# Score products over 64 rows and over 128: the lower parts of the keys in tiles of their own, beside zeros

## The chip, the cores and the metric

The kernel runs on one core of a Trainium2 chip. A core has a matrix engine (TensorE, PE in the profile, its weight loads shown apart as PEld), three engines for element-wise work (VectorE or DVE, ScalarE or ACT, GpSimd or POOL) and one that issues DMAs (SyncE, SP). The metric is the device time of one execution in microseconds (us).

## The reference, cut to what matters

Two layers of an encoder, 512 tokens, model width 1024, all in float32. Each layer is a feed-forward half (SwiGLU, inner width 2816), then three mixers side by side on the same normalised tokens, gated and summed, then a second feed-forward half. The mixers:

```
A: differential attention, 4 heads, two score maps per head over 64 features each
   sc = q[m] . k[m] * 64**-0.5 - slope * |t - s|      (m = 0, 1; 512 x 512)
   o  = softmax(sc[0]) v - lambda * softmax(sc[1]) v
B: windowed attention, 8 query heads, 2 key heads, 64 features, |t - s| <= 128
C: latent attention, 4 heads: sc = qn . kn (128 features) + qpe . kpe (64 rotary features, one kpe for all heads)
```

## The kernel before

Tokens lie along the free dimension (512 columns), features along the 128 partitions. Every float32 operand of a product is split in two parts of a type that TensorE takes in one pass: an upper part (hi, a rounded copy made by ACT) and a lower one (lo, the rest, a subtraction on DVE). A plain product is three products, hi·hi, hi·lo and lo·hi, summed in one PSUM bank (`mm3`, L155 to L157). The weights stream from memory through one queue in chunks of 128x1024 and are split on the way (L71, L72).

Scores over 64 features are done with two products and not three. Two heads (the two maps of A, the two key heads of B) lie in one tile, 64 rows each. `stacked` (L203) makes of the queries one tile per head, with the upper part in the head's own 64 rows and the lower part in the other 64. `doubled` (L217) makes of the keys one tile per head with the upper part in both halves, and one tile `lo` for both heads, each head's lower part in its own 64 rows. `mm_stacked` (L232) then forms the scores of 128 queries:

```
own = slice(m * 64, m * 64 + 64)
self.nc.tensor.matmul(ps, q[:, c], kh, start=start, stop=False)          # L235: 128 rows, (q hi + q lo) . k hi
self.nc.tensor.matmul(ps, q[own, c], kl[own], start=False, stop=stop)    # L236: 64 rows, q hi . k lo
```

In C the 128 unrotated features are three products at L702, and the rotary ones follow by `mm_stacked` into the same bank. The shared rotary key, pk, holds the same 64 features in both halves and is split once (`split`, L240 and L241) into kpeh and kpel.

A mixer runs head by head and step by step (`heads`). In A and C a step is a block of 128 queries against all 512 keys, four steps per head; A has two score maps per step. In B a step is two blocks of queries against the two or three blocks of keys in reach (256 or 384 columns), for two heads, two steps per pair of heads. A step's scores come first; the softmax runs on DVE and ACT (C: L705 to L710); then the step before is finished: its probabilities are transposed (L462), split, and multiplied with the values (L471 to L473, in B L659 to L662). Between the steps stand the projections of the next head and other projections and merges, as filling work. The order written in the code gives priorities; a planner fixes each engine's order of instructions when the program is built, from its own estimate of durations, and each engine keeps that order, waiting where an operand or a buffer isn't ready. POOL does the squares of the norms (L257 to L261, L545), the reciprocal roots (L274) and some sums. Tiles of 128x512 come from one pool of 72 "units"; a new one waits until one is free.

Of the kernel before, what the change touches and what calls it, by code (L numbers as in the profile page):

```python
# [16 lines left out]
P = 128  # L17
D = 1024
T = 512
# [20 lines left out]
class Stream:  # L40
    """The weights, 128 rows by 128 columns at a time, in the order of their use."""

# [44 lines left out]
    def fit(self, width):  # L87
        """Fills a chunk that has no room for so wide a block."""
        while self.pos % CH + width > CH:
            self.order.append((None, P))  # L90
            self.pos += P


class Kernel:
    RAW, AHEAD, WB = 3, 2, 3  # chunks of weights: buffers as loaded, loads ahead, buffers of their parts
    UNITS, PTS = 72, 4  # tiles of 512 and of 1024 columns
    WARM = 8  # products of zeros that raise TensorE's clock while the first loads are under way
    LAG = 1  # steps between the scores of a block of queries and the rest
    FILL0, RATES = (0, 1), (0.35, 0.6, 0.85)  # how much other work goes between an attention's steps

# [11 lines left out]

    # ---- tiles
    def u(self, dt=F32, shape=(P, T), name="u"):
# [26 lines left out]

    # ---- pieces
    def lookup(self, *args, **kw):
        """An activation that needs a table of its own; these keep their order, so that tables change seldom."""
        if self.last is None:
            self.last = self.nc.scalar.activation(*args, **kw)
        else:
            with self.tc.issue_after(self.last.ins):
                self.last = self.nc.scalar.activation(*args, **kw)

    def mm3(self, ps, w, x, start, stop):
        """ps += w^T x, each float32 as the sum of two parts that one pass carries."""
        (wh, wl), (xh, xl) = w, x
        mm = self.nc.tensor.matmul
        mm(ps, wh, xh, start=start, stop=False)  # L155
        mm(ps, wh, xl, start=False, stop=False)  # L156
        mm(ps, wl, xh, start=False, stop=stop)  # L157

    def proj(self, ps, src, xs):
        """128 output features for all tokens; src(k) names a block of weights."""  # L160
        n = len(xs)
        for k in range(n):
            self.mm3(ps, self.w.take(src(k)), xs[k], k == 0, k == n - 1)
# [15 lines left out]
    def group(self, pss, srcs, xs):  # L179
        """Several projections side by side, so that the last of xs is needed late. With no xs,  # L180
        they are made on the way from x."""
        n = len(xs) or NT
        for k in range(n):
            for ps, src in zip(pss, srcs):
                while len(xs) < min(k + (1 if ps is pss[0] else 3), n):
                    xs.append(self.gsplit(self.x[len(xs)], self.g(0, G_FFN1, len(xs)), "h"))
                self.mm3(ps, self.w.take(src(k)), xs[k], k == 0, k == n - 1)
            yield

    def group_rstd(self, pss, srcs, xs, at=(4, 6)):  # L190
        """A group, with the scale of the tokens worked out meanwhile."""
        res = g = None
        for k, _ in enumerate(self.group(pss, srcs, xs), 1):
            if k in at:
                g = g or self.rstd(self.sqacc, D, self.att)
                try:
                    next(g)
                except StopIteration as e:
                    res = e.value
        return res  # L200
# [4 lines left out]
    def stacked(self, src, name):  # L205
        """The parts of two heads' rows, each head's one above the other: the first head's with the
        upper part on top, the second's with the lower one."""
        out = []
# [8 lines left out]
    def doubled(self, src, name):  # L217
        """Of two heads' rows, each head's upper part twice above each other, and the lower parts."""
        out = []
        lo = self.u(F32R, name=name + "l")  # L220
        for m in range(2):
# [5 lines left out]
        for m in range(2):  # L227
            own = slice(m * 64, m * 64 + 64)
            self.nc.vector.tensor_tensor(lo[own], src[own], out[m][own].bitcast(F32), ALU.subtract)
        return out, lo  # L230

    def mm_stacked(self, ps, q, m, c, kh, kl, start, stop):  # L232
        """ps += q^T k over 64 rows: q as stacked, the upper part of k twice above each other."""
        own = slice(m * 64, m * 64 + 64)
        self.nc.tensor.matmul(ps, q[:, c], kh, start=start, stop=False)  # L235
        self.nc.tensor.matmul(ps, q[own, c], kl[own], start=False, stop=stop)  # L236

# [9 lines left out]
    def gsplit(self, src, g, name="g"):  # L247
        """The parts of src times a gain per partition."""
        hi, lo = self.pair(name)
# [13 lines left out]
    def rstd(self, acc, dim, bank, evac=True):  # L263
        """From sums of squares: 1/rms per token, down the partitions and across them. Yields
        where TensorE would wait."""
        nc = self.nc
# [17 lines left out]

    # ---- set-up
    def setup(self):
# [48 lines left out]

    # ---- feed-forward
    def next_h(self, j, gcol):
        """x's tile j is final: its part of the next norm's input."""
        h = None if gcol is None else self.gsplit(self.x[j], gcol, "h")
        if j == 0:  # L340
            self.sqacc = self.u(name="sqacc")
        self.square_sum(self.sqacc, self.x[j], j == 0)
        return h
# [67 lines left out]

    # ---- the three mixers
    def scaled(self, ps, R, by=None):
# [7 lines left out]
    def rproj(self, src, xs, R, by=None):  # L421
        """A projection of normalised tokens: the scale of a token comes after the product."""
        ps = self.acc()
# [6 lines left out]
    def vproj(self, xs, src, out, banks):  # L430
        """Values with tokens down the partitions, 512 features wide."""
        pss = [b("pv") for b in banks]
# [25 lines left out]
    def flip(self, p, n, hi, lo):  # L458
        """The parts of p's transposed blocks; hi and lo take n blocks side by side."""
        ps = self.att("tp")  # L460
# [4 lines left out]
    def pv(self, ps, v, pth, ptl):  # L465
        """ps += values^T probabilities^T over four blocks of keys, for two blocks of queries."""
        mm = self.nc.tensor.matmul
# [7 lines left out]
    def full_pv(self, hd, qb, d, v, st):  # L475
        """Transposes the probabilities of a block of queries; after two blocks, their products with the values."""
        if qb == 0:
# [12 lines left out]
    def heads(self, n, steps, prepare, first, second):  # L490
        """All heads' steps in one line: scores of a step, then the rest of the step before; the
        next head's projections in between. Yields where other work may go."""
        todo = []
# [17 lines left out]
    def branch_a(self, l, h, R, qk, out):  # L511
# [3 lines left out]
        def first(hd, qb):  # L515
# [3 lines left out]
            for m in range(2):  # L519
                self.mm_stacked(pss[m], q[m], m, slice(qb * P, (qb + 1) * P), k[0][m], k[1], True, True)  # L520
            ps = []
# [53 lines left out]
    def vproj_b(self, l, h, R, v):  # L575
        """Values of both key heads, each head's parts side by side."""
        t = yield from self.win(l, [(2176, P)], h, R)
# [16 lines left out]
    def branch_b(self, l, v, kk, h, R, qs, out):  # L594
# [5 lines left out]
        def first(j, hf):  # L600
# [6 lines left out]
            for qi in range(2):  # L607
# [5 lines left out]
                for m in range(2):  # L613
                    self.mm_stacked(pss[m][:, 0:n], q[m], m, slice(qb * P, (qb + 1) * P), kk[0][m][:, ks], kk[1][:, ks], True, True)
                for m in range(2):
# [21 lines left out]
        def second(j, hf, ps):  # L637
# [5 lines left out]
            for m in range(2):  # L643
# [6 lines left out]
                yield  # L650
                # above, the upper parts of the values; below, the lower ones
                side = slice(m * 256, m * 256 + 256)
# [40 lines left out]
    def branch_c(self, l, v, kpe, low, qk, out):  # L693
# [3 lines left out]
        def first(hd, qb):  # L697
# [3 lines left out]
            for i, (a, b) in enumerate(((0, 0), (0, 1), (1, 0))):  # L701
                nc.tensor.matmul(ps, q[a][:, c], k[b], start=i == 0, stop=False)  # L702
            self.mm_stacked(ps, qpe[hd % 2], hd % 2, c, *kpe, False, True)
            nm, s = self.small([P, 1], "cnm"), self.small([P, 1], "cs")
# [35 lines left out]
    def mix(self, l):  # L740
# [26 lines left out]
        z2, z0, z1 = [], [], []  # L767
        # compressed projections of C
        cols = [[(2688 + i * P, P)] for i in range(2)] + [[(2944, 64), (2976, 32), (2944, 32)]] + [[(2304 + i * P, P)] for i in range(3)]
# [34 lines left out]
        nc.tensor.matmul(pk, self.selr, krl, start=False, stop=True)  # L804
        kpe = self.split(pk, "kpe")
        RC, RS = self.u(name="RC"), self.u(name="RS")
# [66 lines left out]
def gather(order, nch, inp):  # L873
    """The weights' blocks, in the order of their use."""
    out = np.zeros((P, nch * CH), np.float32)
# [86 lines left out]
```

## Time and profile before

| | |
|---|---|
| time, median of 3 runs (lowest, highest) | 2548.37 us (2548.07, 2548.67) |
| span of the profiled execution, first to last instruction | 2544.7 us |
| mean granted TensorE clock | 0.998 of full speed |
| PE busy | 2524.1 us, 99% of the span, 11424 products |
| weight loads busy | 2044.0 us, 80% |
| DVE, ACT, POOL busy | 53%, 37%, 11% |
| score products L235 and L236 | 160 of 128 rows, 160 of 64 rows |

The profile is of one execution. PE's busy share says little, because products overlap: a plain one of 512 columns lasts 390 ns in the rows, and the next one starts before it has ended. What a product costs is the time from its start to the next one's start. A row of a timeline gives the start in us, the duration in us, engine, line, operation, tiles (written <- read), the sizes, and in brackets idle time of the engine just before and what ended it; "issue" means that nothing in the profile explains it.

### The profile page before, as it was taken

How to read it: one execution, taken by the hardware profiler on the slowest of the kernel's cores; microseconds unless marked ns; L12 is line 12 of the kernel's file. 1: busy time of each engine (PE TensorE's matmuls, PEld its weight loads, DVE VectorE, ACT ScalarE, POOL GpSimd, SP SyncE). 2: the span in 40 equal slices, each digit the busy share in tenths (PEclk: the TensorE clock that was granted, in tenths of full speed). 3: DMA queues.
4: the chain of work that ended last, by engine and by line, in shares of the span. 5: the costliest groups of instructions: out<-in, count | busy, mean ns of one | idle time of the engine just before them, and what ended most of it. 6: DMA issues, size and time to landing. Idle time of an engine off the chain costs nothing.

```text
span 2544.7 us, 28509 instructions
## 1 busy us (share of the span) xinstructions
PE 2524.1 (99%) x11424; PEld 2044.0 (80%) x11424; DVE 1355.1 (53%) x2004; ACT 936.2 (37%) x1429; POOL 270.6 (11%) x208
## 2 busy tenths in 40 slices
PE   9999999999999999999999999999999999999997
PEld 7888887777777888888888888877777788888886
DVE  6444336666667554443344443366666676544433
ACT  4332223365555433332233322244655553322211
POOL 4000123000001220001100001130000014100011
PEclk9999999999999999999999999999999999999999
DMA  4333332112212233333333333321222122333331
GB/s 159 93 97 100 95 122 86 59 58 75 67 58 67 88 94 100 93 97 100 95 96 100 93 98 99 106 81 51 67 75 66 56 70 89 102 97 94 100 99 67
DMA packets 62484, 223.22 MB, mean 88 GB/s; under 512 B 7200, under 2 KB 7344, under 8 KB 62352
## 3 DMA queue, kind: packets, MB, share of 16 engines
q1 hardware_dynamic: 60912, 217.67, 27.6%
q0 software_dynamic: 864, 2.70, 0.3%
q8 instruction: 89, 1.46, 0.2%
q10 hardware_dynamic: 576, 1.05, 0.1%
q14 instruction: 43, 0.35, 0.0%
HBM read 219.29 MB, written 2.10 MB: 87 GB/s over the span
## 4 chain that ended last, share of the span: by engine, by line
PE 95%; DVE 3%; ACT 1%; issue 1%; POOL 0%; DMA 0%; SPq 0%; DVEq 0%; POOLq 0%; ACTq 0%
PE pa L157 7%; PE pa L155 7%; PE pa L156 7%; PE acc L155 7%; PE po L155 6%; PE po L157 6%; PE po L156 6%; PE acc L156 6%; PE acc L157 6%; PE pg L156 5%; PE pg L155 5%; PE pg L157 5%; PE tp L462 2%; PE pm L155 2%; PE pm L157 2%; PE pm L156 2%
## 5 line engine op out<-in xcount | busy, mean ns | idle before, releaser
L72 DVE TENSOR_TENSOR wlo<-wraw,whi 128x1024 fp32r<-128x1024 f32 (+1 forms) x410 | 526.8, 1285 | 641.9 <-ACT whi L71 640.7
L71 ACT CAST whi<-wraw 128x1024 fp32r<-128x1024 f32 (+1 forms) x410 | 429.7, 1049 | 820.0 <-PE po L156 254.4
L155 PE MATMUL pa<-hh,whi 128*128 128x512 f32 x800 | 312.6, 391 | 0.9 <-DVE x L851 0.9
L157 PE MATMUL pa<-hh,wlo 128*128 128x512 f32 x800 | 311.7, 390 | 1.0 <-DVE wlo L72 1.0
L156 PE MATMUL pa<-hl,whi 128*128 128x512 f32 x800 | 311.7, 390 | 0.0
L155 PE MATMUL acc<-hh,whi 128*128 128x512 f32 x672 | 275.4, 410 | 0.0
L156 PE MATMUL acc<-hl,whi 128*128 128x512 f32 x672 | 263.9, 393 | 0.0
L157 PE MATMUL acc<-hh,wlo 128*128 128x512 f32 x672 | 263.5, 392 | 0.0
L155 PE MATMUL pg<-hh,whi 128*128 128x512 f32 x608 | 236.5, 389 | 0.0
L156 PE MATMUL pg<-hl,whi 128*128 128x512 f32 x608 | 236.5, 389 | 0.0
L157 PE MATMUL pg<-hh,wlo 128*128 128x512 f32 x608 | 236.5, 389 | 0.0
L155 PE MATMUL po<-ah,whi 128*128 128x512 f32 x576 | 224.1, 389 | 0.0
L156 PE MATMUL po<-al,whi 128*128 128x512 f32 x576 | 224.1, 389 | 0.0
L157 PE MATMUL po<-ah,wlo 128*128 128x512 f32 x576 | 224.1, 389 | 0.0
L155 PEld LDWEIGHTS pa<-hh,whi 128*128 128x128 f32 x800 | 150.4, 188 | 33.2 <-DVE x L851 1.3
L157 PEld LDWEIGHTS pa<-hh,wlo 128*128 128x128 f32 x800 | 150.3, 188 | 33.1 <-DVE wlo L72 1.9
L156 PEld LDWEIGHTS pa<-hl,whi 128*128 128x128 f32 x800 | 150.3, 188 | 31.2 <-DVE hl L251 0.3
L155 PEld LDWEIGHTS acc<-hh,whi 128*128 128x128 f32 x672 | 126.3, 188 | 32.5 <-issue 9.0
L157 PEld LDWEIGHTS acc<-hh,wlo 128*128 128x128 f32 x672 | 126.2, 188 | 27.7 <-issue 0.2
L156 PEld LDWEIGHTS acc<-hl,whi 128*128 128x128 f32 x672 | 126.6, 188 | 22.3 <-issue 0.9
L155 PEld LDWEIGHTS pg<-hh,whi 128*128 128x128 f32 x608 | 114.2, 188 | 23.8
L157 PEld LDWEIGHTS pg<-hh,wlo 128*128 128x128 f32 x608 | 114.1, 188 | 23.7
(248 smaller groups left out, 3906.5 us busy)
## 6 DMA issues: line engine op xcount, KB each, us to landing
wraw<-in_w SPq DMA_DIRECT2D x408, 512.0 KB, 3.5
x<-in_x SPq DMA_DIRECT2D x8, 256.0 KB, 6.4
rope<-in_rope POOLq DMA_DIRECT2D x6, 256.0 KB, 3.7
out<-o ACTq DMA_DIRECT2D x4, 256.0 KB, 2.9
out<-o SPq DMA_DIRECT2D x4, 256.0 KB, 3.4
dist<-in_cst POOLq DMA_DIRECT2D x1, 448.0 KB, 4.0
wraw<-in_w SPq DMA_DIRECT2D x1, 384.0 KB, 4.6
lv<-in_lam POOLq DMA_DIRECT2D x1, 256.0 KB, 3.9
```

Of the source, the lines that this page charges most:

```text
L71: self.k.nc.scalar.copy(hi[:, part], r[:, part])
L72: self.k.nc.vector.tensor_tensor(lo[:, part], r[:, part], hi[:, part].bitcast(F32), ALU.subtract)
L155: mm(ps, wh, xh, start=start, stop=False)
L156: mm(ps, wh, xl, start=False, stop=False)
L157: mm(ps, wl, xh, start=False, stop=stop)
L462: self.nc.tensor.transpose(ps[:, i * P:(i + 1) * P], p[:, i * P:(i + 1) * P], self.ident)
```

## The change

`doubled` gives each head's lower part a tile of its own, and the head's other 64 rows of that tile are filled with zeros by POOL (`beside_zeros`). The second product of `mm_stacked` then reads all 128 rows of the stacked queries and of this tile; the queries' lower part meets zeros. C's shared rotary key is no longer split by `split` but into one upper tile and two lower ones, one for each parity of heads, with two subtractions over 64 rows. Nothing else of the program changes; docstrings and comments are dropped.

```diff
     def doubled(self, src, name):
-        out = []
-        lo = self.u(F32R, name=name + "l")
+        out, low = [], []
         for m in range(2):
             t = self.u(F32R, name=name)
             own, other = slice(m * 64, m * 64 + 64), slice(64 - m * 64, 128 - m * 64)
@@
         for m in range(2):
             own = slice(m * 64, m * 64 + 64)
+            lo = self.beside_zeros(m, name + "l")
             self.nc.vector.tensor_tensor(lo[own], src[own], out[m][own].bitcast(F32), ALU.subtract)
-        return out, lo
-
-    def mm_stacked(self, ps, q, m, c, kh, kl, start, stop):
-        own = slice(m * 64, m * 64 + 64)
+            low.append(lo)
+        return out, low
+
+    def beside_zeros(self, m, name):
+        t = self.u(F32R, name=name)
+        self.nc.gpsimd.memset(t[64 - m * 64:128 - m * 64].bitcast(F32), 0.0)
+        return t
+
+    def mm_stacked(self, ps, q, c, kh, kl, start, stop):
         self.nc.tensor.matmul(ps, q[:, c], kh, start=start, stop=False)
-        self.nc.tensor.matmul(ps, q[own, c], kl[own], start=False, stop=stop)
+        self.nc.tensor.matmul(ps, q[:, c], kl, start=False, stop=stop)
@@ branch_a (branch_b and branch_c likewise)
-                self.mm_stacked(pss[m], q[m], m, slice(qb * P, (qb + 1) * P), k[0][m], k[1], True, True)
+                self.mm_stacked(pss[m], q[m], slice(qb * P, (qb + 1) * P), k[0][m], k[1][m], True, True)
@@ mix
-        kpe = self.split(pk, "kpe")
+        kpeh = self.u(F32R, name="kpeh")
+        nc.scalar.copy(kpeh, pk)
+        kpe = kpeh, []
+        for m in range(2):
+            own = slice(m * 64, m * 64 + 64)
+            kpe[1].append(self.beside_zeros(m, "kpel"))
+            nc.vector.tensor_tensor(kpe[1][m][own], pk[own], kpeh[own].bitcast(F32), ALU.subtract)
```

## Rows read from the trace of the kernel before

**Rows 1.** The chain of work that ended last, share of the span by engine.
```profile
PE 95%; DVE 3%; ACT 1%; issue 1%; POOL 0%; DMA 0%; SPq 0%; DVEq 0%; POOLq 0%; ACTq 0%
```

**Rows 2.** Waits of PE: line, waited for, us in total, times, longest.
```profile
PE pr L278 <- POOL r L274: 3.6, 3, 2.1
...
PE cs L702 <- ACT kch L240: 1.4, 2, 1.1
```

**Rows 3.** Timeline, 599.7 to 605.5 us: plain products, then a score pair of A.
```profile
599.70 0.39 PE L157 MATMUL acc<-hh,wlo 128*128 128x512 f32 x1
...
603.33 0.39 PE L235 MATMUL s<-k,q 128*128 128x512 f32 x1
...
603.65 0.50 PE L236 MATMUL s<-kl,q 64*128 64x512 f32 x1
...
604.08 0.49 PE L235 MATMUL s<-k,q 128*128 128x512 f32 x1
...
604.50 0.49 PE L236 MATMUL s<-kl,q 64*128 64x512 f32 x1
...
605.50 0.40 PE L157 MATMUL acc<-hh,wlo 128*128 128x512 f32 x1
```

**Rows 4.** Timeline, 437.4 to 439.0 us: PE and weight loads around a 64-row product of C.
```profile
437.43 0.19 PEld L235 LDWEIGHTS cs<-kpeh,qpe 128*128 128x128 f32 x1
437.65 0.39 PE L235 MATMUL cs<-kpeh,qpe 128*128 128x512 f32 x1
437.97 0.18 PEld L236 LDWEIGHTS cs<-kpel,qpe 64*128 64x128 f32 x1 [0.35 <-issue]
437.97 0.50 PE L236 MATMUL cs<-kpel,qpe 64*128 64x512 f32 x1
...
438.40 0.50 PE L157 MATMUL acc<-ch,wlo 128*128 128x512 f32 x1
...
438.73 0.39 PE L702 MATMUL cs<-kch,qch 128*128 128x512 f32 x1
...
438.96 0.39 PE L702 MATMUL cs<-kcl,qch 128*128 128x512 f32 x1
```

**Rows 5.** Line L236: count, duration ns (min/median/max), starts, forms; the loader's idle time.
```profile
L236 PE MATMUL s<-kl,q x64: 491/497/502, 533.0 to 1959.0; 64*128 64x512 f32 x64
...
L236 PE MATMUL cs<-kpel,qpe x32: 490/497/500, 438.0 to 1790.3; 64*128 64x512 f32 x32
...
  issue: 35.5, 126
```

**Rows 6.** Timeline of PE, 708.2 to 711.8 us: a group of B.
```profile
708.20 0.28 PE L472 MATMUL po<-ptl,vh 128*128 128x256 f32 x1
...
708.79 0.28 PE L235 MATMUL b<-kb,qb 128*128 128x256 f32 x1
...
711.76 0.40 PE L156 MATMUL acc<-hl,whi 128*128 128x512 f32 x1
```

**Rows 7.** POOL's groups by form: shapes, count | busy us, mean ns | idle before.
```profile
L261 POOL TENSOR_TENSOR sqacc<-sqacc,sq 128x512 f32<-128x512 f32 x48 | 81.6, 1700 | 3.7
...
L545 POOL TENSOR_TENSOR osq<-o 128x512 f32<-128x512 f32 x8 | 8.3, 1042 | 413.9 <-ACT o L543 413.9
...
L936 POOL MEMSET const-float32-0.0<- 128x1 f32 x1 | 0.1, 100 | 0.2 <-issue 0.2
```

**Rows 8.** Lines L241 and L229, columns as in rows 5: subtractions of the keys.
```profile
L241 DVE TENSOR_TENSOR kpel<-pk,kpeh x2: 692/692/692, 424.0 to 1685.0; 128x512 fp32r<-128x512 f32 x2
...
L229 DVE TENSOR_TENSOR kl<-t,k x16: 674/687/690, 525.2 to 1914.4; 64x512 fp32r<-64x512 f32 x16
```

**Rows 9.** Timeline, 1711.3 to 1712.0 us: probabilities of a step in C, their transposes.
```profile
1711.34 0.48 DVE L710 TENSOR_SCALAR p<-p,cs 128x512 f32<-128x512 f32 x1
...
1711.97 0.63 PE L462 MATMUL tp<-ident,p 128*128 128x128 f32 x4
```

**Rows 10.** Busy us (instructions) of each engine in C's stretch; clock, DMA share, GB/s.
```profile
437.00:545.00 108.00, 108.00 (x518) 82.90 (x517) 70.90 (x138) 48.44 (x90) 1.30 (x1) 1.00 0.18 54
```

More of the change, by code (lines that the diff above doesn't have):

```diff
@@ L613, in first @@
                 for m in range(2):
-                    self.mm_stacked(pss[m][:, 0:n], q[m], m, slice(qb * P, (qb + 1) * P), kk[0][m][:, ks], kk[1][:, ks], True, True)
+                    self.mm_stacked(pss[m][:, 0:n], q[m], slice(qb * P, (qb + 1) * P), kk[0][m][:, ks], kk[1][m][:, ks], True, True)
                 for m in range(2):
@@ L702, in first @@
                 nc.tensor.matmul(ps, q[a][:, c], k[b], start=i == 0, stop=False)
-            self.mm_stacked(ps, qpe[hd % 2], hd % 2, c, *kpe, False, True)
+            self.mm_stacked(ps, qpe[hd % 2], c, kpe[0], kpe[1][hd % 2], False, True)
             nm, s = self.small([P, 1], "cnm"), self.small([P, 1], "cs")
```

## The prediction

> **What bounds the kernel now.** I read the chain of work that ended last first: TensorE (PE) holds 95% of it [rows 1]. PE's waits for other engines come next: the two longest that concern the mixers are 3.6 and 1.4 us in total [rows 2]. So PE hardly waits, and time saved on PE itself shortens the run. What PE pays for the score products is to be read in a timeline of PE, from start to start, since products overlap. Plain 128-row products of 512 columns start from 599.70 to 603.33 in 16 steps, 3.63 us, 0.227 us each [rows 3]. Around a 64-row product the step changes. In branch C the 128-row product starts at 437.65, the 64-row one at 437.97, the full ones behind it at 438.40, 438.73 and 438.96: steps of 0.32, 0.43, 0.33 and 0.23 [rows 4]. The weight load (PEld) shows why. That of the full L235 starts at 437.43, a whole step ahead of its product; that of the 64-row L236 starts at 437.97 together with it, and for 0.35 us before that the loader waited for nothing that the profile names. This is so everywhere, as the view of line L236 groups it: the products of 512 columns (64 and 32 of them) last 490 to 502 ns, against 0.39 us of a plain one, and the loader's idle time of this kind comes to 35.5 us in 126 spells [rows 5].
>
> **The change, part by part.**
>
> *The 160 lower products become 128 rows high.* C has 32, each alone. From L235 to the second full product behind L236 are four steps, 438.96 - 437.65 = 1.31 us [rows 4]; four plain ones are 0.91. One 64-row product costs 0.40 us too much, and 32 of them 12.8 us. A has 32 pairs, with 128, 64, 128 and 64 rows in turn. From 603.33 to 605.50 are six steps, 2.17 us against 1.36, so 0.81 too much [rows 3], and 32 x 0.81 = 25.9 us. B has 16 groups of four pairs, two of 256 columns and two of 384. From the first at 708.79 to 711.76, the second full product behind them, are nine steps: four of 256, four of 384 and one of 512 columns, 2.97 us [rows 6]. A plain step of 256 columns is (708.79 - 708.20) / 5 = 0.118 us; for 384, which never stands plain, 0.172 is my estimate, half way from 0.118 to 0.227. So 4 x 0.118 + 4 x 0.172 + 0.227 = 1.39 us would do, 1.58 is too much, and 16 x 1.58 = 25.3 us. Sum: 64.0 us. It can't be more if plain steps are the best that there is; it is not less than the loader's 35.5 us, unless rival 1 or 2 holds. I take 64.0: the steps count what the order of products lost, the loader's idle only a part of it.
>
> No row shows a product with zeros in half of its rows, but the form, 128 rows by 512 columns, is that of L235, which starts 0.23 us behind the product before it, its load ahead [rows 4].
>
> A page speaks against this. The Trainium skill (TensorE: Matmul & The Clock Gate, Part 3: Packing small matmuls — row/col tiling) says that a weight load overlaps running products only where it goes to another group of rows. By that rule the 64-row products have the better overlap, full ones have none, and the change saves nothing. The trace disagrees: the load that runs ahead goes into the same 128 rows as the product under way, and the one that stands still is the 64-row one [rows 4].
>
> *24 fills with zeros on POOL:* two for each of eight heads of A, two for B's keys and two for C's in each layer, 16 + 4 + 4. The only fills in the trace are 128x1, 0.10 us; the costliest group of 128x512 operations on POOL has a mean of 1.70 us [rows 7]. So 2.4 to 40.8 us of POOL, and no gain, since nothing is taken from POOL. What hides them: a fill needs no input but a free tile, and POOL idles most of the time; its eight squares of A's outputs (L545) alone have 413.9 us of idle time before them [rows 7]. I take 0 on the path, the near end, since the tile is asked for a projection before its scores. If that cover is gone, a fill holds a head's first lower product, and behind it all of PE, at up to 1.70 us each, 40.8 us. Behind a fill on POOL's queue stand the norms' reciprocal roots (L274), and PE waits for these already, 3.6 us in three places [rows 2].
>
> *C's shared key: one subtraction of 128 rows becomes two of 64.* The one has 692 ns, a 64x512 one of the key heads 687 [rows 8]: half the rows are not cheaper, so 0.69 us more on DVE per layer. This lies shortly before C's first scores, where PE waits for ACT's kch, 1.4 us in two waits [rows 2], and kch comes behind DVE. The bounds are 0, if DVE makes it up in a gap, and 1.4 us, both layers in full; a gain is excluded, as it only adds. I take the middle, 0.7 us. The subtractions in `doubled` were of 64 rows before; only their target is another tile, 0.
>
> *What is late next.* A step's scaled probabilities p must be ready before their transposes. In C that is tight in places: p is written from 1711.34 to 1711.82 and the transposes start at 1711.97, with 0.15 us to spare [rows 9]. PE gets there up to 0.40 us earlier, of which 0.25 would be lost here; were all 32 steps so tight, 8.0 us, and if none, 0. PE's waits name no p today [rows 2]; a quarter of the steps seems ample to me, 2.0 us. In A and B more other work stands between, 0; the bound for those is rival 1.
>
> *Tiles.* Each `doubled` and C's key hold one more of the 72 unit tiles. None of PE's longest waits is for a free tile [rows 2]; I take 0, and the far end is rival 3.
>
> The sum is -64.0 + 0 + 0.7 + 2.0 = -61.3 us. The span becomes 2544.7 - 61.3 = 2483.4. The median of the runs, 2548.4, is 3.7 us above the span of the profiled execution, and this stays: 2487 us.
>
> **Rivals.**
>
> 1. *The softmax takes most of it back.* In A and C PE comes to the transposes early and waits there for all that it saved. 12.8 + 25.9 us go, B's 25.3 stay: 2523 us. For it: the 0.15 us in [rows 9]. Against: in C's stretch DVE is busy 70.9 of 108 us, ACT 48.4 [rows 10], so both can follow a PE that is a few per cent faster.
>
> 2. *The load of a 128-row score product isn't hidden either*, because what stalls is a product into a bank of sums just written, or a load into rows in use, and not the change of height. Then a step stays near 0.42 us and the time at 2548: the change doesn't do what it says. For it: in A's pairs the second 128-row product, at 604.08, comes 0.43 us behind the first lower one [rows 3]. Against: C's L702 and L235 go into one bank, with 0.23 us between them [rows 4]. (The rule of the skill's page above, on groups of rows, gives this case as well.)
>
> 3. *Slower: POOL's queue holds the zeros back.* POOL works in order. A fill queued behind the square of an A head's output (L545) waits with it, 413.9 / 8 = 51.7 us each [rows 7]. A head has four steps, so a fill that is one step late holds the next head's first lower product 12.9 us, and PE behind it: eight heads, 103 us, 2548.4 - 61.3 + 103 = 2590 us. From 61.3 / 8 = 7.7 us a head it decides the sign. A fill that gets no free tile does the same. Against: in the code the fill stands ahead of that square, a projection before its scores.
>
> **How the numbers follow.** The forecast has 0.87, rival 1 0.06, rival 2 0.03, rival 3 0.04. Some 0.2% (5 us) can't be told from no change here. Faster is 0.87 + 0.06 = 0.93, same 0.03, slower 0.04. The range: the edits give the planner another order to find, and I allow 6 us either way for it, a little over the 5.0 us of waits in [rows 2]. Below, nothing is lost: 2548.4 - 64.0 - 6 = 2478. Above, the far ends of the two small terms: 2548.4 - 64.0 + 8.0 + 1.4 + 6 = 2500. Outside stay the rivals with 0.13 and a little of the forecast's own.
>
> **What would show it.** In the profile after, the lower score products have the rows of the upper ones (128x512, 0.39 us), and the loader's 35.5 us of idle time before them are gone. C's four steps are 0.23 each; A's six add up to 1.36 us. In each layer A, B and C are shorter by about 13.0, 12.7 and 6.4 us, and the feed-forward parts are as before. Waits of PE for p at the transposes would speak for rival 1, steps of 0.42 us between 128-row score products for rival 2, waits at the lower products for POOL's zeros for rival 3. I am wrong if the full load doesn't run ahead in the pairs, or if PE's waits grow by more than 10 us.

## The result, and the profile after

The changed kernel takes 2488.95 us (median of 4 runs, 2488.62 to 2489.62) against 2548.22: 59.3 us less, a ratio of 0.9768 with a 95% interval from 0.9754 to 0.9782. The forecast was 2487.

Start with the same score products in the timeline of PE after the change (`mm_stacked` is L243 and L244 now, C's other products L710). First a lower product of C, with the weight loads.

```profile
440.08 0.19 PEld L243 LDWEIGHTS cs<-kpeh,qpe 128*128 128x128 f32 x1
440.31 0.39 PE L243 MATMUL cs<-kpeh,qpe 128*128 128x512 f32 x1
440.31 0.19 PEld L244 LDWEIGHTS cs<-kpel,qpe 128*128 128x128 f32 x1
440.54 0.39 PE L244 MATMUL cs<-kpel,qpe 128*128 128x512 f32 x1
...
440.77 0.39 PE L710 MATMUL cs<-kcl,qch 128*128 128x512 f32 x1
...
441.00 0.39 PE L710 MATMUL cs<-kch,qcl 128*128 128x512 f32 x1
```

The load of L244 starts at 440.31, a step ahead of its product, and has no idle time in front of it. The steps are 0.23 throughout, where [rows 4] had 0.32, 0.43 and 0.33. A score pair of A and the products behind it, the answer to [rows 3]:

```profile
533.91 0.39 PE L243 MATMUL s<-k,q 128*128 128x512 f32 x1
534.14 0.39 PE L244 MATMUL s<-kl,q 128*128 128x512 f32 x1
534.36 0.39 PE L243 MATMUL s<-k,q 128*128 128x512 f32 x1
534.59 0.39 PE L244 MATMUL s<-kl,q 128*128 128x512 f32 x1
...
535.27 0.39 PE L157 MATMUL acc<-hh,wlo 128*128 128x512 f32 x1
```

Six steps take 1.36 us (2.17 before). And a group of B, the answer to [rows 6]:

```profile
696.82 0.33 PE L243 MATMUL b<-kb,qb 128*128 128x384 f32 x1
...
698.24 0.39 PE L156 MATMUL acc<-hl,whi 128*128 128x512 f32 x1
```

Nine steps, 1.42 us (2.97 before; the plain steps that I had estimated made 1.39). In these rows a pair of A gives back 0.81 us, a group of B 1.55 and a product of C 0.40: 32 x 0.81 + 16 x 1.55 + 32 x 0.40 = 63.5 us.

The stretches of the three mixers can be measured too. PE has the same number of products between the same two marks before and after (528 in C's, 820 in A's, 631 in B's stretch of a layer):

| stretch, from start to start on PE | before, layers 1 and 2 (us) | after | shorter, both layers |
|---|---|---|---|
| C: first product of pk (the shared key) to A's first score | 112.1, 111.8 | 105.2, 105.1 | 13.5 |
| A: from there to B's first score | 176.3, 175.9 | 164.8, 163.8 | 23.6 |
| B: from there to B's last product with the values | 131.1, 130.6 | 119.9, 119.1 | 22.7 |

The sum is 59.8 us; A and B give less than their steps (25.9 and 24.8), C a little more. Part of what A and B miss shows in the waits of the weight loader, whose list has smaller waits than PE's own. Of before (waits view of PEld: waiting line, waited for, us in total, times, longest):

```profile
PEld s L236 <- issue: 17.8, 63, 0.4
PEld acc L155 <- issue: 10.2, 44, 0.2
PEld cs L236 <- issue: 9.6, 27, 0.4
PEld b L236 <- issue: 8.0, 36, 0.3
PEld s L235 <- issue: 7.3, 30, 0.2
...
PEld po L471 <- ACT pth L240: 2.9, 14, 0.5
...
PEld po L472 <- DVE ptl L241: 1.4, 5, 0.3
...
PEld pob L659 <- ACT bth L240: 1.1, 4, 0.4
...
PEld pob L660 <- DVE btl L241: 0.8, 2, 0.6
```

And of after:

```profile
PEld po L479 <- ACT pth L248: 4.1, 16, 0.6
PEld po L480 <- DVE ptl L249: 3.2, 10, 0.5
...
PEld pob L667 <- ACT bth L248: 2.3, 6, 0.5
PEld pob L668 <- DVE btl L249: 1.6, 3, 1.2
...
PEld tp L470 <- issue: 1.2, 5, 0.3
```

Every "issue" wait at a score product is gone (the list goes down to 0.2 us); what is left of the kind stands at the transposes (L470). The waits for the split transposes (pth, ptl, bth, btl) have gone from 2.9 + 1.4 + 1.1 + 0.8 = 6.2 us to 4.1 + 3.2 + 2.3 + 1.6 = 11.2. The list names no wait for p or for a fill.

The fills themselves, by form on POOL (shapes, count | busy us, mean ns | idle before and what ended it):

```profile
L237 POOL MEMSET kl<- 64x512 f32 x16 | 8.3, 520 | 121.1 <-PE tp L470 118.6 <-PE cs L710 2.0
L237 POOL MEMSET kbl<- 64x512 f32 x4 | 2.1, 521 | 0.2
```

0.52 us each, and 24 of them 12.5 us. But A's fills stood 118.6 us in POOL's queue until, by this view, transposes had set a tile free: the tiles are scarce, and POOL bears it.

The span fell by 57.2 us only, from 2544.7 to 2487.5, because the profiled execution of before was the quicker one while the first weights were loading. PE's busy time in the first 20 us, before and then after:

```profile
0.00:20.00 20.00, 17.51 (x61) 12.80 (x62) 14.29 (x14) 11.55 (x16) 13.96 (x13) 1.00 0.77 265
```

```profile
0.00:20.00 20.00, 15.73 (x55) 11.47 (x56) 13.83 (x13) 10.32 (x14) 13.73 (x14) 1.00 0.72 244
```

Six products fewer, 6 x 0.227 = 1.4 us, in a stretch that the change doesn't touch. The first product of pk, ahead of all scores, starts at 420.5 before and at 422.8 after; in seven of the eight runs below it starts between 421.6 and 422.8, so it is before that stands apart. The 59.3 us of the medians are the number to explain.

### The profile page after: what moved, and what is told of

Same layout as the page of the kernel before. It is cut to its first block, busy times and chain, and to the rows that moved or that the text cites. A ratio compares the mean times of both kernels' runs of the same rounds, so it can differ in the third digit from the quotient of the medians.

```text
span 2487.5 us, 28555 instructions
## 1 busy us (share of the span) xinstructions
PE 2464.2 (99%) x11424; PEld 2043.2 (82%) x11424; DVE 1350.7 (54%) x2006; ACT 931.0 (37%) x1429; POOL 282.5 (11%) x232
## 4 chain that ended last, share of the span: by engine, by line
PE 94%; DVE 3%; ACT 2%; issue 1%; POOL 0%; DMA 0%; SPq 0%; DVEq 0%; ACTq 0%; POOLq 0%
PE pa L157 7%; PE pa L155 7%; PE pa L156 7%; PE po L156 6%; PE po L157 6%; PE po L155 6%; PE acc L155 6%; PE acc L156 6%; PE acc L157 6%; PE pg L157 6%; PE pg L155 6%; PE pg L156 6%; PE tp L470 2%; PE pm L155 2%; PE pm L156 2%; PE pm L157 2%
## 5 line engine op out<-in xcount | busy, mean ns | idle before, releaser
L155 PE MATMUL pa<-hh,whi 128*128 128x512 f32 x800 | 312.6, 391 | 1.7 <-DVE x L865 0.9
L155 PE MATMUL acc<-hh,whi 128*128 128x512 f32 x672 | 269.5, 401 | 0.0
L155 PE MATMUL pg<-hh,whi 128*128 128x512 f32 x608 | 236.5, 389 | 0.0
L155 PE MATMUL po<-ah,whi 128*128 128x512 f32 x576 | 224.1, 389 | 0.0
L155 PEld LDWEIGHTS pa<-hh,whi 128*128 128x128 f32 x800 | 150.2, 188 | 33.8 <-ACT whi L71 1.9
L155 PEld LDWEIGHTS acc<-hh,whi 128*128 128x128 f32 x672 | 126.4, 188 | 22.6
L156 PEld LDWEIGHTS pg<-hl,whi 128*128 128x128 f32 x608 | 114.0, 188 | 23.8
```

## The experiments

Theory S (switch): a change of height between one product and the next, 128 rows to 64 or back, keeps the next weight load from running ahead, and a 64-row product among full ones pays for two such changes. Rival P (product): a 64-row product is dear by itself, wherever it stands. Then four runs for the small terms.

**e1, two 64-row products in a row** (kernel before):

```diff
+        self.nc.tensor.matmul(ps, q[own, c], kl[own], start=False, stop=False)
         self.nc.tensor.matmul(ps, q[own, c], kl[own], start=False, stop=stop)
```

> The kernel before, with each 64-row lower product (L236) issued twice in a row into the same sums, so the lower part counts twice; 160 products more. Theory S (switch): the 0.40 us is the price of two changes of height, from 128 rows to 64 and back; a second 64-row product behind the first needs no change and costs a plain step: 96 x 0.227 + 32 x 0.118 + 32 x 0.172 = 31 us, so about 2579 us. Rival P (product): every 64-row product, or its weight load, costs 0.40 us more than a 128-row one wherever it stands: 31 + 64 = 95 us, about 2643 us.

Measured 2584.62 us against 2547.86, 36.8 us more (ratio 1.0151, 1.0133 to 1.0169). Theory S had 31, P 95. Timeline of PE around a doubled lower product of C:

```profile
438.79 0.40 PE L235 MATMUL cs<-kpeh,qpe 128*128 128x512 f32 x1
439.12 0.50 PE L236 MATMUL cs<-kpel,qpe 64*128 64x512 f32 x1
439.46 0.39 PE L237 MATMUL cs<-kpel,qpe 64*128 64x512 f32 x1
439.78 0.50 PE L157 MATMUL acc<-ch,wlo 128*128 128x512 f32 x1
...
440.35 0.40 PE L703 MATMUL cs<-kcl,qch 128*128 128x512 f32 x1
```

From L235 to the third full product behind are 1.56 us, 0.25 more than the same stretch of [rows 4]: the second 64-row product adds a plain step and 0.02 us, and not 0.63. Its load is no longer late either; the loader's "issue" idle at its line is 0.2 us in all 160:

```profile
L237 PE MATMUL cs<-kpel,qpe x32: 385/393/491, 439.5 to 1815.2; 64*128 64x512 f32 x32
its engine sat idle before it (us, times) until:
  issue: 0.2, 1
```

Part of the 36.8 us is the clock. In the profiled execution (2586.12 us) TensorE's granted clock was at half, 1.2 in place of 2.4 GHz, in three stretches of B, 10.3 us together, each right behind a group of B's scores with the 64-row products doubled. One of them (columns as in [rows 10]; the clock is the 0.51):

```profile
807.50:810.90 3.40, 3.40 (x9) 2.72 (x9) 0.79 (x5) 2.54 (x8) 0.01 (x1) 0.51 0.00 0
```

Plain steps of 512 columns are 0.43 us there and not 0.227, so by estimate some 5 us were lost. No other profile here has such a stretch in the mixers, and the four runs of e1 go with their mean granted clock: 2582.8 and 2583.1 us at 0.997, 2586.1 at 0.996, 2591.4 at 0.993. By steps, which leave this out, the doubled products add 0.47 us to a pair of A, 0.59 to a group of B and 0.24 to a product of C: 32 x 0.47 + 16 x 0.59 + 32 x 0.24 = 32 us, where S had 31.

**e2, the control with two 128-row products** (changed kernel):

```diff
+        self.nc.tensor.matmul(ps, q[:, c], kl, start=False, stop=False)
         self.nc.tensor.matmul(ps, q[:, c], kl, start=False, stop=stop)
```

> The changed kernel, with each lower product (now 128 rows) issued twice in a row, so the lower part counts twice. Both theories: a plain step each, 31 us, about 2520 us. It is the control of the experiment with two 64-row products: the difference of the two additions is what a 64-row product costs beside another one.

Measured 2516.75 us, 27.8 more than the changed kernel (ratio to before 0.9881, 0.9866 to 0.9896). By the medians the second 64-row product cost 36.8 / 160 = 0.23 us and the second 128-row one 27.8 / 160 = 0.17, over a mix of widths whose plain mean is 0.19. The first number holds e1's lost clock, and the second a quick start: in e2's profile the first product of pk comes 3.2 us earlier than in the changed kernel's. In the three mixers alone e1's trace is 38.4 us longer than that of before, some 33 without the clock, and e2's 30.5 longer than the changed kernel's, so 0.21 and 0.19 us a product. P falls; S stands.

**e3, the two lower products of a pair side by side** (kernel before, in A and B):

```diff
-            for m in range(2):
-                self.mm_stacked(pss[m], q[m], m, c, k[0][m], k[1], True, True)
+            for part in range(2):          # 0: upper, 128 rows; 1: lower, 64 rows
+                for m in range(2):
+                    self.mm_part(part, pss[m], q[m], m, c, k[0][m], k[1])
```

> The kernel before, with the four products of a score pair of A and B in another order: both upper ones (128 rows), then both lower ones (64 rows, first rows 0 to 63, then rows 64 to 127, into two banks of sums); C as before. Theory S: half of the changes of height go in A and B, 25.9 / 2 + 25.3 / 2 = 25.6 us, about 2523 us. Theory S with the two 64-row products running side by side: a plain step less for each pair too, 32 x 0.227 + 16 x 2 x (0.118 + 0.172) / 2 = 12 us, about 2511 us. Rival P: nothing changes, 2548 us.

Measured 2514.47 us, 33.4 less than before (0.9872, 0.9857 to 0.9887). Half of the switches explains 25.6 us; the rest asks for the two 64-row products to run at once. For that the forecast was 2511 us; 3.5 us of it are missing. Timeline, PE and loads, of a pair of A (L241 upper, L243 lower; x2 is two products in one row):

```profile
539.60 0.41 PEld L241 LDWEIGHTS s<-k,q 128*128 128x128 f32 x2
539.83 0.61 PE L241 MATMUL s<-k,q 128*128 128x512 f32 x2
540.37 0.19 PEld L243 LDWEIGHTS s<-kl,q 64*128 64x128 f32 x2 [0.35 <-issue]
540.37 0.50 PE L243 MATMUL s<-kl,q 64*128 64x512 f32 x2
540.80 0.19 PEld L155 LDWEIGHTS acc<-hh,whi 128*128 128x128 f32 x1 [0.25 <-issue]
...
541.37 0.40 PE L157 MATMUL acc<-hh,wlo 128*128 128x512 f32 x1
```

Two loads together take 0.19 us and two 64-row products 0.50, as long as one, and the full product behind starts 0.43 us after them, as behind a single one [rows 4]. The six steps are 1.54 us: 2.17 less one change there and back (0.40) less one step (0.23). That is theory S with both products side by side, to 0.01 us in this pair. Over the whole of A and B, stretch by stretch, the run is 33.5 us shorter, less than such steps add up to, as in the changed kernel.

**e4, all score products over 64 rows** (kernel before):

```diff
-        self.nc.tensor.matmul(ps, q[:, c], kh, start=start, stop=False)
+        self.nc.tensor.matmul(ps, q[own, c], kh[own], start=start, stop=False)
```

> The kernel before, with the upper score product (L235) over 64 rows as well: it leaves the lower part of the queries out. In A a pair is now 64, 64, 64, 64 rows, first two in rows 0 to 63 and then two in rows 64 to 127. Theory S: the changes inside the pairs and groups go, one entry and one exit per pair of A (32 x 0.40 stay of 25.9 us) and per group of B (16 x 0.40 stay of 25.3 us), C keeps its 12.8: 13.1 + 18.9 = 32 us less, about 2516 us; if a change from the rows 0 to 63 to the rows 64 to 127 costs a switch too, 0.2 us x 32 and 0.2 us x 48 come back, about 2532 us. Rival P: 160 more dear products, 64 us more, about 2612 us.

Measured 2504.63 us, 43.2 less than before (0.9832, 0.9818 to 0.9847), below both of S's numbers. A pair of A in PE's timeline:

```profile
540.95 0.50 PE L235 MATMUL s<-k,q 64*128 64x512 f32 x2
541.29 0.40 PE L236 MATMUL s<-kl,q 64*128 64x512 f32 x2
541.62 0.50 PE L155 MATMUL acc<-hh,whi 128*128 128x512 f32 x1
...
542.19 0.39 PE L157 MATMUL acc<-hh,wlo 128*128 128x512 f32 x1
```

The two maps run side by side in the two halves: four products in 0.67 us. Both upper products start at 540.95, though the code gives both products of the first map before those of the second; whether the planner or the engine put them so, the trace doesn't say. So the order that I had priced, one half and then the other, didn't run here, and no price of a change of half shows. P, which wanted 64 us more, falls again. By my estimate this isn't a way to a faster kernel: with the queries' lower part, which is left out here, a pair needs a third round. In B's groups of this run a round of two products inside a 64-row stretch is a plain step (0.17 us for 384 columns, 0.11 for 256), so a third round would add some 0.23 us: 1.24 + 0.23 = 1.47 us from a pair's first score to the third full product behind, against 1.36 in the changed kernel. No run tests it.

**e5, C's part of the change alone** (kernel before, with C's shared key and C's scores as in the changed kernel):

> The kernel before with C's part of the change alone: the shared rotary key in one upper and two lower tiles beside zeros, C's lower product over 128 rows; A and B keep their 64-row products. By the terms of the prediction: -12.8 for 32 changes of height there and back, +0.7 for the longer subtraction, +2.0 for the softmax, so -10.1 us, about 2538 us. Rival, that the two small terms don't exist: -12.8 us, 2535 us; the waits of PE in C's stretch then stay as they were.

Measured 2534.82 us against 2548.17, 13.4 less (0.9947, 0.9935 to 0.9960). That is the rival's -12.8 and not the terms' -10.1, though the interval (about 3 us to each side) just reaches both. The trace decides it: C's stretch is 13.5 us shorter over both layers, and A's and B's are as before to 0.1 us. The loader's waits for kch at C's start are no longer than before either, 1.0 us in place of 2.3.

**e6, zeros filled once; e7, its control; e8, every fill four times** (changed kernel):

```diff
# e6
-        t = self.u(F32R, name=name)
-        self.nc.gpsimd.memset(t[64 - m * 64:128 - m * 64].bitcast(F32), 0.0)
-        return t
+        ring = self.zeroed[m]              # three tiles per half, filled in setup_mix
+        ring.append(ring.pop(0))
+        return ring[-1]
# e6 and e7
-    UNITS, PTS = 72, 4
+    UNITS, PTS = 66, 4
# e8
+        for _ in range(4):
             self.nc.gpsimd.memset(t[64 - m * 64:128 - m * 64].bitcast(F32), 0.0)
```

> The changed kernel with six tiles for lower parts, three per half, filled with zeros once, early in the first layer's mixers, and used in turn; 18 fills go, and the pool has 66 unit tiles in place of 72. Theory: the fills are hidden, so the same time, 2489 us within 0.2%. Rival 3 of the prediction in a small form, that POOL's queue or the waits for a free tile cost PE something: up to 5 us faster.

> The changed kernel with 66 unit tiles in place of 72. It is the control of the run with the zeros filled once, and it asks how near a shortage of tiles is. Theory: the fills wait for tiles on POOL for 118.6 us in the changed kernel, and PE isn't held; six tiles fewer make this longer and still cost PE little, 2489 to 2499 us. Rival 3: a shortage holds the heads' first lower products, 7.7 us a head in eight heads, 60 us slower.

> The changed kernel with each fill of zeros done four times: 72 fills more of 0.52 us, 37 us more on POOL. Theory: hidden behind the projections, the same time within 0.2%, 2489 us, at most 3 us more at C's start, where POOL's rotary factors stand behind two fills. Rival: the fills are on the path, 72 x 0.52 = 37 us more, 2526 us.

Measured: e6 2489.01 us (ratio to before 0.9766, 0.9753 to 0.9780), the changed kernel's time with as many tiles in all (66 and six). e8 2489.84 (0.9771, 0.9758 to 0.9784): POOL is busy 320.7 us where it was 282.5, 38.2 more, and the time moved by 0.9, less than can be told from nothing. In e8's trace A's and B's stretches are as long as in the changed kernel, and C's is 1.5 us longer over both layers, within the 3 that I had allowed at its start. The fills are off the path. e7 2494.97 us (0.9791, 0.9778 to 0.9805), 6.0 more than the changed kernel: six tiles fewer, and it is B that pays. Its stretch (busy us of PE, PEld, DVE, ACT, POOL) in the changed kernel and in e7:

```profile
692.80:812.70 119.90, 118.89 (x634) 100.79 (x632) 89.86 (x216) 73.36 (x165) 12.40 (x10) 1.00 0.22 71
```

```profile
692.00:814.50 122.50, 119.78 (x634) 100.24 (x632) 91.00 (x216) 73.87 (x165) 12.39 (x10) 1.00 0.22 69
```

The same 634 products take 2.6 us longer in this layer and, between the same marks, 4.1 in the second, with new waits of the loader in B, for the maxima of the scores and for B's outputs:

```profile
PEld tp L470 <- DVE bnm L627: 3.8, 7, 1.1
...
PEld pob L667 <- DVE ob L674: 2.8, 4, 1.1
```

So a shortage of tiles is near, at six of 72, and its price is a tenth of what rival 3 needed. No run is faster than the changed kernel beyond its spread.

## Why the prediction was right, point by point

*PE bounds, and time saved on it shortens the run:* right. The chain is PE for 94% after the change as well.

*64.0 us from steps:* right in mechanism and size. The same steps measured after give 63.5; A and C came out to the digit, B's 1.58 per group was 1.55, since the nine plain steps took 1.42 us and not the 1.39 that I had estimated. (In A and C my sum goes to the third full product behind the scores, not to the second as it says, in B to the second; the step between is plain, so the excess is the same.) The lower bound of 35.5 us, the loader's "issue" idle before L236, was too low for a reason worth keeping: the same change of height also delays the upper products and the products behind (L235 and L155 in the loader's list), and the steps count all of them.

*The rule that full-height loads don't overlap running products* (the Trainium skill, TensorE: Matmul & The Clock Gate, Part 3): as its list of what overlaps puts it, it does not hold here. In the changed kernel the score products are full and their loads run a step ahead (440.31 for the product at 440.54). The same Part also lets a load go ahead into a background weight buffer; that would fit, but no run here shows such a buffer. The other half of the rule holds: loads to different groups of rows do overlap, two in 0.19 us beside the two products in e3. Another page had the mechanism. The Trainium skill (TensorEngine Tiling (Array Packing), Tiling Modes, Key Properties) says that changing the tiling mode, and not just the tile, drains the engine. For tiles of 64 rows the traces agree: e1 (same mode, a plain step) and e4 (another tile of the same mode, no cost) against 0.40 us for a change there and back. For tiles of 64 columns no such price shows (last section).

*Fills, 0 on the path:* right, shown by e8 and e6. The size, 0.52 us, lay inside my wide bounds.

*C's longer subtraction, 0.7 us, and the transposes of C, 2.0 us:* not seen. C's stretch gave 13.5 us in the changed kernel and in e5, no less than its steps of 12.8. The two subtractions do take 0.69 us each, but nothing waits longer for them, and PE still doesn't wait for p.

*A and B, 0 lost behind the scores:* this step was wrong, and by somewhat more than the former two were too dear. The steps give 25.9 + 24.8 = 50.7 us in A and B. Their stretches are 46.3 us shorter, 11.8 and 11.4 a layer where I had announced 13.0 and 12.7, and the medians leave 59.3 - 13.4 = 45.9, so 4.4 to 4.8 us were lost. The loader's waits for the split transposes grew by 5.0 us, at the products with the values, one stage behind the place that I had looked at. Not all of this reaches PE, whose steps that end at these products (400 in A and B) grew by 2.6 us in sum; in e5, where A's and B's scores are as before, they didn't grow. Most of the rest is that scores and the two products behind them gave 48.4 us and not 50.7; in A only 19 of the 32 pairs stand among full products as in [rows 3]. Why the split transposes come late is argued, not shown: with less time of PE between, ACT's and DVE's split ends last a little more often, and no run takes these waits away. That the errors nearly cancelled is luck: the sum was 61.3, the measured 59.3.

*Rivals.* 1, the softmax takes most: no; the loader waits for no p, and what A and B lack is a tenth of their gain, in part one stage later. 2, no gain: no. 3, POOL holds the zeros back: its cause exists (118.6 us of fills waiting for tiles on POOL), but it reaches no score; e7 shows the first few us of it.

## What to carry to other kernels

Price a matmul by start-to-start steps over the whole neighbourhood until steps are plain again, not by its duration or by one idle column. Where short products stand singly among full ones, zeros up to the full height cost PE nothing and save a change of height there and back, 0.40 us here; where two short products can stand next to each other in different halves of the rows, they run at once, and then it depends on how many stand between two changes. Filling with zeros is cheap in time on an idle engine, but its tiles are not: count them first. And before a difference between two runs is divided by a count, look at the granted clock and the start of both: in e1 and e2 these were worth 3 to 5 us.

## What the runs showed of the hardware that I had not expected

Two 64-row products in different halves and different banks ran at once, weight loads included (e3: two in 0.50 us; e4: four in 0.67 us, and in B two of 256 columns in one plain step of 0.11). Two in the same half and the same bank did not (e1: a step of 0.34 us and a next one of 0.32); whether rows or bank decide is open, no run separates them.

A change in the columns shows no price: B's products with the values have 128 rows and 64 columns of weights among full ones, and their steps are 0.11 to 0.12 us, plain for 256 columns. From PE's timeline after the change:

```profile
711.66 0.28 PE L667 MATMUL pob<-bth,vb 128*128 128x256 f32 x1
711.78 0.28 PE L668 MATMUL pob<-btl,vb 128*64 128x256 f32 x1
711.89 0.28 PE L667 MATMUL pob<-bth,vb 128*128 128x256 f32 x1
```
